# One store of eight output tiles cut into 32 transfers from two queues, with the rows of eight partitions divided differently

## The chip, the core and the metric

The kernel runs on one core of a Trainium2 chip. The core has a matrix engine (TensorE, PE in the profile), two engines for elementwise work (VectorE, DVE, and ScalarE, ACT), a programmable engine (GpSimd, POOL), a queue processor (SyncE, SP), and 16 DMA engines that carry data between the chip's memory (DRAM) and the on-chip memory SBUF, which has 128 partitions. Products are accumulated in a second on-chip memory, PSUM. The metric is the time of one launch in microseconds (us), lower is better; a median of a few runs is given.

## What is computed

`x` has 16 x 1024 rows of 512 floats, `weight` is 512 x 768, `gamma` has 512 entries (all ones here) and `eps` is 1e-5.

```python
rms = np.sqrt(np.mean(x ** 2, axis=-1, keepdims=True) + eps)
x_norm = x / rms * gamma
return np.matmul(x_norm, weight).astype(np.float32)
```

The kernel flattens `x` to 16,384 rows. It reads 16,384 x 512 x 4 B = 33.6 MB, and writes 16,384 x 768 x 4 B = 50.3 MB.

## The kernel before

**Tiles.** The 16,384 rows are 128 tiles of 128 rows; a tile has one row in each partition. For a tile, GpSimd casts the rows to bf16, the tile is turned (by TensorE with an identity, line 230, and copied out of PSUM by VectorE, line 239; for some tiles by VectorE's own 32x32 transposes, line 271), TensorE multiplies it with the bf16 weights (line 300), and ScalarE (even tiles, line 279) or VectorE (odd tiles, line 281) scales the 768 results of each row by the row's 1/rms on their way from PSUM into an output buffer `ot`. The row's sum of squares is formed beside this by ScalarE (line 196).

**Groups and buffers.** Output tiles are gathered in groups of eight. `ot` has three buffers of eight tiles; group g uses buffer g % 3. So the first tile of a group can be written only when the store of the group three before has landed. Groups 1 to 13 (tiles 8 to 111) are each stored by one transfer of eight tiles, 3,072 KB. At the two ends groups are cut smaller: tiles 112 to 127 leave as 4, 4, 4, 2 and 2 tiles.

**How a store lies in memory.** `rows` (line 140) gives partition p a stretch of consecutive rows of the output, so the eight tiles of a group are, in each partition, 8 x 768 floats = 24,576 bytes in one piece in DRAM, and also one piece in `ot`. A store of a group is 128 such pieces.

**Order and queues.** The program is written as a list of operations in one order (class `Order`). `emit` (line 39) walks the list once, works out which earlier operations each one has to wait for, and issues each to its engine's own queue with those waits ahead of it. A transfer gets a semaphore of its own, or takes over that of an earlier transfer that its queue is known to have seen finished (lines 64 to 70). All stores and the first loads are issued by SyncE, later loads by ScalarE; GpSimd issues no transfer. `store` (line 288) is called after each tile's scaling and issues a transfer when the last tile of its group has been written. A queue is in order: SyncE, while it waits for the tiles of one store, issues nothing else.

**The end of the program.** The transfers that nobody in the program waits for (the last stores) are collected; ScalarE waits for all of them but the last one (lines 438 to 440), and the last store, of tiles 126 and 127, is issued by SyncE behind everything else (lines 441 to 446). The program ends when all have landed.

```python
def store(i):
    first, n = o_first[i], o_size[i]
    s = first // OG % 3
    if i == first + n - 1:
        src = ot[s][:, first % OG:first % OG + n, :]
        order.transfer(SP, lambda: SP.dma_start(out=rows(out, first, n), in_=src), reads=cells("ot", s, first % OG, n))
```

Of the kernel before, what the change touches and what calls it, by code (L numbers as in the profile page):

```python
# [20 lines left out]
class Order:  # L21
# [17 lines left out]
    def emit(self):  # L39
        nc = self.tc.nc  # L40
        streams = {id(e): n for n, e in enumerate((nc.tensor, nc.vector, nc.scalar, nc.gpsimd, nc.sync))}
        writer, readers = {}, {}
        known = [dict() for _ in streams]
        clocks, needs, place, slot_of, slots = [], [], [], {}, []
        count = [0] * len(streams)
        for n, (proc, engine, _, reads, writes) in enumerate(self.ops):
            at = streams[id(engine)]
            if proc is None:
                me, turn = ("transfer", n), 1
            else:  # L50
                count[at] += 1
                me, turn = at, count[at]
            written = {writer[cell] for cell in reads + writes if cell in writer}
            read = {d for cell in writes for d in readers.get(cell, ())}
            need = []
            for d in sorted(written | read, reverse=True):
                who, when = place[d]
                if who == me and (engine is nc.tensor or d not in written):
                    continue
                if known[at].get(who, 0) < when:  # L60
                    need.append(d)
                    for k, v in clocks[d].items():
                        known[at][k] = max(known[at].get(k, 0), v)
            if proc is None:
                free = [k for k, d in enumerate(slots) if known[at].get(("transfer", d), 0)]
                if free:
                    slots[free[0]] = n
                else:
                    slots.append(n)
                slot_of[n] = ("slot", slots.index(n))  # L70
            clock = dict(known[at])
            clock[me] = turn
            place.append((me, turn))
            clocks.append(clock)
            needs.append(need)
            for cell in reads:
                readers.setdefault(cell, []).append(n)
            for cell in writes:
                writer[cell], readers[cell] = n, []
        awaited = {d for need in needs for d in need}  # L80
        seen = {who for clock in known for who in clock}
        last = [n for n, (me, _) in enumerate(place) if me not in seen and not isinstance(me, int)]
        sems, marks, done = {}, {}, {}
        for n in range(len(self.ops)):
            me = slot_of.get(n, place[n][0])
            if n in slot_of or n in awaited:
                if me not in sems:
                    sems[me] = self.tc.alloc_semaphore(f"done{len(sems)}")
                done[me] = done.get(me, 0) + (16 if n in slot_of else 1)
                marks[n] = (sems[me], done[me])  # L90
        for n, (proc, engine, issue, _, _) in enumerate(self.ops[:-1]):
            for d in needs[n]:
                engine.wait_ge(*marks[d])  # L93
            ins = issue()
            if n in marks:
                ins.then_inc(marks[n][0], 16 if n in slot_of else 1)
        return [marks[n] for n in last if n < len(self.ops) - 1], self.ops[-1][2]
# [3 lines left out]
def kernel(  # L101
# [8 lines left out]
    nc = tc.nc  # L110
    PE, DVE, ACT, POOL, SP = nc.tensor, nc.vector, nc.scalar, nc.gpsimd, nc.sync
    order = Order(tc)
# [5 lines left out]
    out = out.flatten_outer_dims()  # L118
    N, D = x.shape
    _, O = out.shape  # L120
    K = D // P
    NT = N // P
    NP = NT // 2
    XG, OG = 16, 8
# [15 lines left out]
    def rows(ap, i, n):  # L140
        base, t = (i - i % OG, OG) if OG <= i < XG else (x_first[i], x_size[i]) if i < OG else (i - i % XG, XG) if i < 2 * XG else (i - i % (2 * XG), 2 * XG)
        return ap[base * P:(base + t) * P, :].rearrange("(p t) d -> p t d", t=t)[:, i - base:i - base + n, :]

    def sb(name, shape, dtype):
        return nc.alloc_sbuf_tensor(name, shape, dtype).ap()
# [14 lines left out]
    ot = [sb(f"ot{n}", [P, OG, O], F32) for n in range(3)]  # L160
# [7 lines left out]
    def cells(name, slot, i, n=1):  # L168
        return [(name, slot, t) for t in range(i, i + n)]
# [115 lines left out]
    def accumulator():  # L285
        return next(turns) % 3

    def store(i):
        first, n = o_first[i], o_size[i]
        s = first // OG % 3  # L290
        if i == first + n - 1:
            src = ot[s][:, first % OG:first % OG + n, :]
            order.transfer(SP, lambda: SP.dma_start(out=rows(out, first, n), in_=src), reads=cells("ot", s, first % OG, n))

    def hold(lhsT, cell):
# [21 lines left out]
    def finish_tile(i, a, engine):  # L317
        s = i // OG % 3

        before = [("ot", s, i % OG - 1)] if i == o_first[i] + o_size[i] - 1 else []  # L320
        scale(engine, ot[s][:, i % OG, :], ops[a][:, :O], rstd[:, i:i + 1],
              [("ops", a, 0), ("ops", a, 1), ("rstd", i)] + before, [("ot", s, i % OG)])
        store(i)
# [158 lines left out]
```

## Time and profile before

| What | Value |
|---|---|
| Median of 3 runs | 208.95 us (208.85 to 216.69) |
| The profiled execution's own time | 209.07 us |
| Span from its first to its last instruction | 207.1 us |
| PE, DVE, ACT, POOL busy, share of the span | 94%, 72%, 70%, 29% |
| Granted PE clock, mean | 0.993 |
| Moved by DMA | 85.62 MB, 413 GB/s over the span |
| Packets on SyncE's queue, on ScalarE's queue | 4,320 and 1,732 |
| Last GpSimd instruction begins | 171.44 us |
| Store of tiles 104 to 111 is issued | 177.86 us |
| Last store is issued, lands | 200.40 us, 206.16 us |

The profile is one execution. Times within it count from its first instruction. "Issued" is the time at which the queue's processor handed the transfer over; "landed" is when the transfer's semaphore reached its full count. That semaphore is raised in 16 steps, and the trace has the time of each. The trace also has each DMA packet with its start, length and size, but not which of the 16 DMA engines carried it. The DMA share in a table of windows is the time of all packets that began in the window, divided by the window and by 16, so 1.00 means that all 16 engines are at work and 0.06 that one is. An engine that is busy in the page need not be the one that others wait for; the chain of waits and the windows show that.

### The profile page before, as it was taken

To read this page: it belongs to the slowest core of one execution; us is meant where nothing else is said; L and a number is where in the kernel's file an instruction comes from. 1 tells how busy PE (TensorE), PEld (TensorE's weight loads), DVE (VectorE), ACT (ScalarE), POOL (GpSimd) and SP (SyncE) were. 2 spreads that over 40 slices of the span, in tenths; PEclk is the share of its full clock that TensorE was granted. 3 is DMA by queue.
4 is the path that set the end of the run, shared out by engine and by line. 5 is a ranking of instruction groups with operands and counts; after the bars stand their busy time and mean duration, and the time that the engine had idled before them with its cause. 6 is when DMAs were issued, how large, how long until landed. Compare 5 with 4: busy or idle time off the path is not lost.

```text
span 207.1 us, 2794 instructions
## 1 busy us (share of the span) xinstructions
PE 194.7 (94%) x1236; PEld 72.7 (35%) x717; DVE 149.5 (72%) x255; ACT 144.3 (70%) x343; POOL 60.0 (29%) x34
## 2 busy tenths in 40 slices
PE   7789999999999999999999999999999989999940
PEld 1233434343334334433344333443343324333310
DVE  0446556999579975999579975999569964999530
ACT  4598898777777687777777687676949758683310
POOL 2156752157006340065105170060604224000000
PEclk9999999999999999999999999999999999999997
DMA  6999999999999999999999999999999999999992
GB/s 222 402 434 453 370 419 420 426 461 407 437 429 423 449 419 440 419 434 429 432 449 411 430 434 423 445 423 437 413 424 445 427 440 435 423 437 394 394 412 120
DMA packets 6064, 85.62 MB, mean 413 GB/s; under 512 B 674, under 2 KB 676, under 8 KB 1828
## 3 DMA queue, kind: packets, MB, share of 16 engines
q1 hardware_dynamic: 4320, 60.30, 68.9%
q10 hardware_dynamic: 1732, 25.17, 28.5%
q8 instruction: 7, 0.11, 0.2%
q14 instruction: 5, 0.04, 0.0%
HBM read 35.13 MB, written 50.33 MB: 413 GB/s over the span
## 4 chain that ended last, share of the span: by engine, by line
PE 71%; DMA 17%; DVE 5%; SPq 1%; issue 1%; POOL 1%; ACT 0%; ACTq 0%
PE ps L300 63%; DMA out_dram<-ot 12%; PE ps L230 8%; DMA xt<-in_x_dram 5%; DVE ot L281 2%; DVE xTq L271 2%; DVE xT L239 1%; POOL xb L188 1%; SPq L345 0%; ACT ot L279 0%; SPq L177 0%; DVE rstd L203 0%; SPq L477 0%; ACTq L93 0%; SPq L436 0%
## 5 line engine op out<-in xcount | busy, mean ns | idle before, releaser
L300 PE MATMUL ps<-w_bf,xT 128*128 128x512 bf16 (+1 forms) x800 | 147.9, 326 | 2.1 <-DVE w_bf L281 1.1
L279 ACT ACTIVATE ot<-ps,rstd 128x768 f32<-128x768 f32 x64 | 57.6, 899 | 48.5 <-PE ps L300 37.3
L196 ACT ACTIVATE jk<-xt 128x512 bf16<-128x512 f32 x128 | 78.7, 619 | 1.9 <-DMA xt<-in_x_dram 1.9
L188 POOL CAST xb<-xt 128x2048 bf16<-128x2048 f32 (+3 forms) x21 | 46.4, 2218 | 112.4 <-PE ps L230 69.0
L281 DVE TENSOR_SCALAR ot<-ps,rstd 128x768 f32<-128x768 f32 x64 | 64.8, 1013 | 9.5 <-PE ps L300 8.1
L296 PEld LDWEIGHTS <-xT 128*128 128x128 bf16 x400 | 39.3, 98 | 60.7 <-issue 52.8
L230 PE MATMUL ps<-ident_f,xb 128*128 128x128 f32 x200 | 54.4, 276 | 0.9 <-POOL xb L188 0.9
L239 DVE COPY xT<-ps 128x1024 bf16<-128x1024 bf16 (+1 forms) x53 | 34.5, 654 | 24.2 <-PE ps L230 22.5
L271 DVE STREAM_TRANSPOSE xTq<-xq 32x256 f32<-32x256 f32 x112 | 48.8, 435 | 3.4
L230 PEld LDWEIGHTS ps<-ident_f,xb 128*128 128x128 f32 x200 | 28.3, 143 | 46.6 <-issue 43.3
L300 PE MATMUL ps<-w_bf,xTq 128*128 128x512 bf16 x224 | 42.8, 326 | 0.0
L196 ACT ACTIVATION_READ_ACCUMULATOR jk<-xt 128x1 f32 x128 | 24.4, 190 | 0.0
L296 PEld LDWEIGHTS <-xTq 128*128 128x128 bf16 x112 | 11.0, 98 | 14.5 <-issue 14.5
L260 POOL CAST xq<-xt 128x2048 bf16<-128x2048 f32 x7 | 13.3, 1893 | 0.0
L203 DVE RECIPROCAL rstd<-rms 128x8 f32<-128x8 f32 (+3 forms) x20 | 3.9, 193 | 8.1 <-ACT rms L201 7.9
L201 ACT ACTIVATE rms<-ssq,eps_sb 128x8 f32<-128x8 f32 (+3 forms) x20 | 6.0, 300 | 0.6
L300 PE MATMUL ps<-warm 128*128 128x512 bf16 x10 | 4.5, 588 | 1.4 <-DVE eps_sb L354 1.4
L279 ACT ACTIVATE w_bf<-w_f,g_sb 128x768 bf16<-128x768 f32 x2 | 1.9, 935 | 1.8 <-DMA w_f<-in_weight_dram 1.8
L377 DVE COPY g_sb<-ps 128x4 f32<-128x4 f32 x1 | 0.2, 163 | 3.2 <-PE ps L371 3.2
L341 ACT ACT_TABLE_LOAD x1 | 1.3, 1283 | 1.5 <-SPq L436 1.5
L281 DVE TENSOR_SCALAR w_bf<-w_f,g_sb 128x512 bf16<-128x512 f32 (+2 forms) x3 | 1.4, 482 | 1.2 <-DMA w_f<-in_weight_dram 1.2
L371 PEld LDWEIGHTS ps<-ident_f,g_row 2*128 2x128 f32 x2 | 0.3, 200 | 2.6 <-issue 2.6
(10 smaller groups left out, 2.0 us busy)
## 6 DMA issues: line engine op xcount, KB each, us to landing
out_dram<-ot SPq DMA_DIRECT2D x13, 3072.0 KB, 22.7
xt<-in_x_dram ACTq DMA_DIRECT2D x12, 2048.0 KB, 18.8
xt<-in_x_dram SPq DMA_DIRECT2D x3, 2048.0 KB, 18.2
out_dram<-ot SPq DMA_DIRECT2D x4, 1536.0 KB, 10.9
out_dram<-ot SPq DMA_DIRECT2D x3, 768.0 KB, 6.8
w_f<-in_weight_dram SPq DMA_DIRECT2D x2, 768.0 KB, 5.9
xt<-in_x_dram SPq DMA_DIRECT2D x2, 512.0 KB, 5.4
xt<-in_x_dram SPq DMA_DIRECT2D x1, 1024.0 KB, 9.5
```

The lines of the kernel that those rows point to most:

```text
L188: run(POOL, lambda: POOL.tensor_copy(out=xb[s][:, i % 8:i % 8 + n, :], in_=src), of, cells("xb", s, i % 8, n))
L196: run(ACT, lambda: ACT.activation(out=jk[j], in_=src[:, 0, :], func=AF.Square, accum_out=ssq[:, i:i + 1]), of, [("jk", j), ("ssq", i)])
L201: run(ACT, lambda: ACT.activation(out=rms[:, s], in_=ssq[:, s], func=AF.Sqrt, scale=1.0 / D, bias=eps_sb), [("ssq", t) for t in range(i, i ...
L203: run(DVE, lambda: DVE.reciprocal(out=rstd[:, s], in_=rms[:, s]), [("rms", i)], [("rstd", t) for t in range(i, i + n)])
L230: run(PE, lambda: PE.transpose(out=tp[b][:, t, h, :], in_=words[:, lo:lo + P], identity=ident_f), cells("xb", s, j % 4 * 2 + t) + ["ident" ...
L239: run(DVE, lambda: DVE.tensor_copy(out=dst[:, t:t + n, :], in_=src[:, t:t + n, :]), [("tp", b)], cells("xT", j % 4, t, n))
L260: run(POOL, lambda: POOL.tensor_copy(out=xq[s], in_=src), of, [("xq", s)])
L271: run(DVE, lambda: DVE.transpose(out=dst, in_=src), [("xq", s)], [("xTq", s)])
L279: run(ACT, lambda: ACT.mul(out=dst, in_=src, mul=r), reads, writes)
L281: run(DVE, lambda: DVE.tensor_single_scalar(out=dst, in_=src, scalar=r, op=mybir.AluOpType.mult), reads, writes)
L296: run(PE, lambda: PE.ldweights(lhsT), [cell])
L300: run(PE, lambda: PE.add_instruction(mybir.InstMatmult(name=nc.get_next_instruction_name(), engine=mybir.EngineType.PE, ins=[PE.lower_ap(r ...
```

## The change

The store of one group, tiles 104 to 111 (`first == NT - 24`, group 13), is no longer one transfer of SyncE. A new function `spread` issues 32 transfers, 16 on SyncE and 16 on GpSimd, in eight rounds. A round p takes:

- on SyncE, the seven partitions p, p+4, ..., p+24, whole rows (7 x 24,576 B);
- on GpSimd, the partition p+28, the first 384 of the 768 columns of each of its eight rows (8 pieces of 1,536 B);
- on GpSimd, the eight partitions p+64, p+68, ..., p+92, whole rows (8 x 24,576 B);
- on SyncE, the partition p+28, the other 384 columns (8 pieces of 1,536 B).

Over the rounds p = 0 to 3 and 32 to 35 this covers all 128 partitions once. The partitions that are taken apart are 28 to 31 and 60 to 63. In `emit`, a transfer that GpSimd issues always gets a semaphore of its own. All other stores, the loads and the computation are as before, and so is the number of bytes.

```diff
             if proc is None:
                 free = [k for k, d in enumerate(slots) if known[at].get(("transfer", d), 0)]
-                if free:
+                if free and engine is not nc.gpsimd:
                     slots[free[0]] = n
                 else:
                     slots.append(n)
...
+    def spread(dst, src, held):
+
+        def part(engine, p, n, cols=slice(0, O)):
+            at = slice(p, p + 4 * n - 3, 4)
+            order.transfer(engine, lambda: engine.dma_start(out=dst[at, :, cols], in_=src[at, :, cols]), reads=held)
+
+        for p in (0, 1, 2, 3, 32, 33, 34, 35):
+            part(SP, p, 7)
+            part(POOL, p + 28, 1, slice(0, O // 2))
+            part(POOL, p + 64, 8)
+            part(SP, p + 28, 1, slice(O // 2, O))
+
     def store(i):
         first, n = o_first[i], o_size[i]
         s = first // OG % 3
         if i == first + n - 1:
             src = ot[s][:, first % OG:first % OG + n, :]
+            if first == NT - 24:
+                spread(rows(out, first, n), src, cells("ot", s, first % OG, n))
+                return
             order.transfer(SP, lambda: SP.dma_start(out=rows(out, first, n), in_=src), reads=cells("ot", s, first % OG, n))
```

## The prediction, made before the changed kernel was run

> **What bounds the kernel now.** I read the page's busy shares and slices first, then the end of the chain of waits, then windows of the last microseconds.
>
> ```profile
> PE 194.7 (94%) x1236; PEld 72.7 (35%) x717; DVE 149.5 (72%) x255; ACT 144.3 (70%) x343; POOL 60.0 (29%) x34
> ...
> PE   7789999999999999999999999999999989999940
> ...
> POOL 2156752157006340065105170060604224000000
> PEclk9999999999999999999999999999999999999997
> DMA  6999999999999999999999999999999999999992
> ```
>
> TensorE and the DMA engines are both full almost throughout, the clock is granted, and GpSimd (POOL) is empty in the last six slices. With two candidates the end has to be looked at by itself. The chain ends with matmuls of line 300 to 199.06 and this:
>
> ```profile
> 199.09 1.02 DVE ot L281
> ```
>
> The last tile is scaled at 200.11, its store is issued at 200.40 and lands 5.8 us later, at 206.16. What are these 5.8 us? Windows after the issue (stretch, length, busy time of PE, PEld, DVE, ACT, POOL, PE clock, DMA share, GB/s):
>
> ```profile
> 200.00:203.20 3.20, 0.00 (x0) 0.00 (x0) 0.10 (x1) 0.00 (x0) 0.00 (x0) 1.00 1.02 419
> 203.60:204.60 1.00, 0.00 (x0) 0.00 (x0) 0.00 (x0) 0.00 (x0) 0.00 (x0) 0.83 0.06 25
> 204.60:205.60 1.00, 0.00 (x0) 0.00 (x0) 0.00 (x0) 0.00 (x0) 0.00 (x0) 0.50 0.06 25
> ```
>
> Until 203.2 all sixteen DMA engines work; from 203.6 to 205.6 the share is 0.06, one sixteenth: **one DMA engine alone holds up the end**. The semaphore steps agree: fifteen of the last store's land at 203.60 to 203.79, the sixteenth at 206.16, 2.37 us later. The lag is old: behind the fifteenth it was 1.31 us in the store issued at 142.43, 1.94 at 166.14, 2.23 at 177.86. From one landing to the next (176.08, 183.65, 191.19) this engine needed 7.57 us for its share of 3,072 KB, the fifteenth (174.46, 181.71, 188.96) 7.25. What a lighter load on it can give is these **2.37 us, 1.1%**, and no more; a measurement of this kernel tells about 2% from no change.
>
> **The change, part by part.** The store as it was, issue and landing:
>
> ```profile
> 177.86 0.33 SPq L293 DMA_DIRECT2D out_dram<-ot  x1
> ...
> out_dram<-ot SPq DMA_DIRECT2D x1, 3072.0 KB, 13.3
> ```
>
> Its buffer (group 13, buffer 1) is not used again, so no compute instruction waits for it, before or after; if it lands late, only the end is late. I follow the DMA engines in three classes, and take for this that partitions 28 to 31 and 60 to 63 are the late engine's share.
>
> (1) That engine gives up 7.57 us and gets an eighth of eight rows: 16 pieces of 1,536 B. The packet records show 121 ns for 3,072 B, so 0.061 us each, 0.98 us in all. It is 6.6 us less loaded, far over its lag, and falls in with the others.
>
> (2) Seven engines keep their 24,576 B a round on SyncE and get the same 0.98 us on top. Idle time hides it: in every store seven engines are early (store of 142.43: seven steps to 165.49, eight from 166.34 to 166.62, one at 167.93), and near 191 and again before 196 they run dry:
>
> ```profile
> 195.00:195.90 0.90, 0.90 (x8) 0.24 (x3) 0.00 (x0) 0.72 (x1) 0.00 (x0) 1.00 0.75 314
> ```
>
> With 16 engines at 0.75 over 0.9 us, some 3.6 engine-us are idle; the count of packets under way falls to 8. If that cover were gone, this class would end 0.98 us later and cap the gain at 1.4 us. Their feed keeps pace if two SyncE issues take under the 1.03 us of work that a round brings. SyncE's nearest row:
>
> ```profile
> 2.47 2.49 SPq L177 DMA_DIRECT2D xt<-in_x_dram  x5
> ```
>
> Five issues back to back, 0.50 us each, of which 0.33 is the instruction in later rows. The new ones have 7 or 8 pieces where those have 128. I take 0.42 us, between 0.33 and 0.50: 16 of them last until 177.86 + 6.7 = 184.6. Behind them in SyncE's queue stands the store of tiles 112 to 115, issued at 184.07 before: 0.5 us late (none at 0.33; 1.8 us at 0.50).
>
> (3) Eight engines carry partitions 64 to 127 and get this store from GpSimd alone. GpSimd is free: its last cast begins at 171.44 and ends at 173.33. But a round takes it two transfers, of c us each, and brings each engine 0.91 us of work (24,576 B; 912 ns in 1,540 of 1,664 packets). These engines have earlier work until about 181.15 (their landings of 181.36 to 181.71, less the 0.48 us by which the late engine's last landing, 206.16, follows its last packet, 205.68). After that they starve in part, until the next full-width store arrives. **c is the unknown of this change**: no GpSimd transfer is in the trace. From below, SyncE's issue of the same operation, 0.33 us. From above, GpSimd's usual instruction:
>
> ```profile
> L260 POOL CAST xq<-xt x7: 1893/1893/1894, 30.3 to 171.4; 128x2048 bf16<-128x2048 f32 x7
> ...
> 10.04 1.04 POOL L188 CAST xb<-xt 128x1024 bf16<-128x1024 f32 x1 [4.51 <-DMA xt<-in_x_dram]
> ```
>
> Those work through 1,024 to 2,048 elements a partition, and the shortest casts (512 elements) take 0.61. A transfer has 8 pieces to describe, so I take the middle of the two short casts, **c = 0.8**. From issue to first packet I use 1.0 us (first load: issued 0.94, first packet 1.98; the store of 194.93: engines back at work at 195.9). The eight engines' 24,576 B arrive at 177.9 + 1.6 k + 1.0 = 180.5, 182.1, 183.7, 185.3 and so on, the next store at 184.6 + 1.0 = 185.6. They work 181.15 to 182.06, 182.1 to 183.0, 183.7 to 184.6, and from 185.3: 1.44 us idle. About 0.2 of it would have been idle before 195.9 anyway. So this class ends 1.24 us later than the fifteen did.
>
> ScalarE's 32 further waits at the end cost nothing: a passed wait is 0.02 us (a chain row of line 93), 0.6 us in all, and ScalarE has nothing else to do from 198.68 to the landing at 206.16.
>
> The sum, on the profiled execution's own time (209.07; 1.97 of it outside the span): 209.07 - 2.37 + 1.24 = 207.94. That execution is 0.12 above the median of the runs, 208.95; I say **207.9 us**, a gain of 0.5%.
>
> [...]
>
> **Rivals.** (A) The sum above, with c from 0.33 to 1.2: at 0.4 there is no idle time and all of 2.37 goes, 206.6; at 1.2 the arrivals are 2.4 us apart and the eight engines are idle for 2.4 us, which gives it all back. Own range 206.5 to 208.9.
>
> (B) Slower: GpSimd feeds too slowly. Place: the eight engines after 181. It decides from c = 1.2, where idle time passes 2.37 + 0.2. Up to c = 1.6 the loss stays under 1.2 us, since the later stores fill the gaps; beyond, the last of the 16 transfers itself arrives after the rest. At c = 1.9 that is 177.9 + 30.4 + 1.0 = 209.3, with 0.91 of work 210.2 against 205.68: +4.5, so 213.5. For it: the median cast is 1.89. Against: the pieces are few.
>
> (C) The pieces land elsewhere. If GpSimd's 8-row transfers fell on the same eight engines that SyncE uses, those would get 7.27 us more, of which idle time hides some 2: 203.4 + 0.98 + 7.27 - 1.8 = 209.9 against 205.68, +4.2, or 213.1. No row tells which engine takes which row of a short transfer.
>
> (D) It doesn't do what it says: the late engine is another one. No packet record names its engine. Then the late one keeps its 7.57 us and adds 0.98, since it has no idle time: 209.9; if it is one of the eight of (3), its backlog to 183.2 covers most of the starving and it loses 0.5: 209.5.
>
> **Chances.** A 0.60, B 0.20, C 0.08, D 0.12. Faster by over 2% (under 204.8) asks for more than the lag there is: 0.01. Slower by over 2% (over 213.1): B from c = 1.87, 0.05, and half of C, 0.04, with 0.01 for hidden costs of the new queue: 0.10. Within 2%: 0.89. The range goes from all of the lag gone, 206.5, to GpSimd at its usual cast, 213.5.
>
> **What would show it.** In the changed profile: the lone 0.06 after 203.6 is gone; the last store's sixteen steps land within some 0.5 us, or a group of eight is last, which is B's sign. GpSimd's sixteen transfers would be a row between 178 and 191 with c as their spacing, the DMA share from 181 to 186 near 0.85, and SyncE's store of tiles 112 to 115 at 184.6. A last store with one step 2 us behind would show D; seven or eight engines some 6 us behind, C. I would be wrong above all through c, and if the short transfers cost the DMA engines more than their bytes.

## The result: slower by 4%

The changed kernel took 218.05 us (median of 4 runs, 217.82 to 218.17), the kernel before, on the same chip, 209.28 us (median of 4, 208.85 to 216.69). The ratio is **1.0425, 95% interval 1.0397 to 1.0453**. Forecast were 207.9 us and a range from 206.5 to 213.5. The 216.69 is an execution in the chip's slower state and is not in the ratio.

The profiled execution took 218.09 us, its span is 216.3 us. From its page, the lines that answer to those shown of before:

```profile
PE 194.3 (90%) x1212; PEld 72.8 (34%) x717; DVE 149.6 (69%) x255; ACT 143.7 (66%) x343; POOL 68.3 (32%) x50
...
PE   7899999999999999999999899998999999999000
...
POOL 3236660552023600633032600624033607700000
PEclk9999999999999999999999999999999999999955
DMA  6999999999999999999999999999999996546994
...
q0 software_dynamic: 512, 1.67, 2.1%
...
L292 POOL DMA_DIRECT2D out_dram<-ot x16 | 8.3, 527 | 6.2 <-DVE ot L281 6.2
```

TensorE's busy time is that of before (194.3 against 194.7). New are a dip of the DMA row, "6546", over some 20 us, and three slices at the end without TensorE where before there was one. GpSimd's sixteen transfers took 8.3 us together to issue, 527 ns each. The chain of waits still ends with the last tile, but what follows it is now much longer:

```profile
200.57 0.02 issue
200.60 1.02 DVE ot L281
```

The tile is scaled at 201.62 (before 200.11), its store lands at 215.20 (before 206.16). Why so late is told by SyncE's own timeline (start, length, queue, line, operation, count; a merged row covers the time from the first to the last of its issues):

```profile
168.57 0.33 SPq L308 DMA_DIRECT2D out_dram<-ot  x1
179.37 17.81 SPq L292 DMA_DIRECT2D out_dram<-ot  x16
197.23 5.07 SPq L308 DMA_DIRECT2D out_dram<-ot  x5
```

Sixteen short issues keep SyncE from 179.37 to 197.18, 1.11 us each. The store of tiles 112 to 115, ready long before, goes out at 197.23; in the kernel before it went at 184.07:

```profile
184.07 0.33 SPq L293 DMA_DIRECT2D out_dram<-ot  x1
```

GpSimd's timeline of the changed kernel ends sooner:

```profile
179.65 8.29 POOL L292 DMA_DIRECT2D out_dram<-ot  x16 [6.22 <-DVE ot L281]
```

What the DMA engines do meanwhile is in windows of the changed kernel (stretch, length, busy PE, PEld, DVE, ACT, POOL, then PE clock, DMA share, GB/s):

```profile
180.00:184.00 4.00, 3.95 (x27) 1.62 (x16) 3.69 (x8) 3.08 (x8) 4.00 (x9) 1.00 0.54 199
184.00:188.00 4.00, 4.00 (x28) 1.59 (x16) 3.84 (x8) 3.04 (x10) 3.94 (x8) 1.00 0.55 213
188.00:192.00 4.00, 3.95 (x27) 1.44 (x15) 3.80 (x7) 1.40 (x2) 0.00 (x0) 1.00 0.50 199
192.00:196.00 4.00, 4.00 (x26) 1.17 (x12) 3.27 (x6) 1.30 (x2) 0.00 (x0) 1.00 0.46 190
196.00:200.00 4.00, 3.95 (x26) 1.21 (x13) 1.43 (x2) 1.60 (x2) 0.00 (x0) 1.00 0.63 256
200.00:204.00 4.00, 0.56 (x4) 0.06 (x1) 1.02 (x1) 0.20 (x1) 0.00 (x0) 1.00 1.05 439
```

and of the kernel before, for the second and fourth of these:

```profile
184.00:188.00 4.00, 4.00 (x28) 1.58 (x16) 3.80 (x9) 2.36 (x5) 0.00 (x0) 1.00 0.95 409
...
192.00:196.00 4.00, 4.00 (x27) 1.22 (x13) 2.27 (x3) 1.72 (x2) 0.00 (x0) 1.00 0.94 396
```

**Half of the DMA engines stand idle from about 182 to 198.** The share is a half, and the rate is a half too (199 GB/s at 0.54, against 409 at 0.95). In the packet records at most eight packets of data are under way at a time from 183.2 to 198, mostly eight or seven (a ninth for 0.13 us in all; from 182 to 183.2 it is mostly nine). The engines at work carry SyncE's short transfers, and GpSimd's as well: had the 8-row transfers of GpSimd gone to the other eight, these would have shown. Then the wide store comes, all sixteen work at 1.05, and the end is one lone engine again:

```profile
213.80:214.80 1.00, 0.00 (x0) 0.00 (x0) 0.00 (x0) 0.00 (x0) 0.00 (x0) 0.50 0.05 18
```

Fifteen of the last store's steps land at 213.44 to 213.62, the sixteenth at 215.20. The lag that the change was about is still there: 1.58 us, where it was 2.37.

**Where the 9 us are.** The last landing moved by 215.20 - 206.16 = 9.04 us, in four parts along the path:

| Part | before | after | difference |
|---|---|---|---|
| store of tiles 104 to 111 issued | 177.86 | 179.37 | +1.51 |
| from there to the store of tiles 112 to 115 | 6.21 | 17.86 | +11.65 |
| from there to the fifteenth step of the last store | 19.72 | 16.39 | -3.33 |
| from the fifteenth step to the sixteenth | 2.37 | 1.58 | -0.79 |

The first part lies ahead of the change: in this execution the tiles had already fallen behind before the split; why, and whether the other three did, is open. The second is the loss. The third says how much of a late issue is hidden: before, the engines had 3.3 us of earlier work in front of these stores; now they have none.

### The profile page after: what moved, and what is told of

It is laid out like the page before. It is cut to its first block, busy times and chain, and to the rows that moved or that the text cites. A ratio compares the mean times of both kernels' runs of the same rounds, so it can differ in the third digit from the quotient of the medians.

```text
span 216.3 us, 2817 instructions
## 1 busy us (share of the span) xinstructions
PE 194.3 (90%) x1212; PEld 72.8 (34%) x717; DVE 149.6 (69%) x255; ACT 143.7 (66%) x343; POOL 68.3 (32%) x50
## 4 chain that ended last, share of the span: by engine, by line
PE 59%; DMA 29%; DVE 2%; issue 1%; ACT 1%; SPq 1%; POOL 0%; ACTq 0%
PE ps L315 52%; DMA out_dram<-ot 24%; PE ps L230 7%; DMA xt<-in_x_dram 4%; DVE ot L281 1%; ACT ot L279 1%; POOL xb L188 0%; SPq L360 0%; SPq L177 0%; DVE xT L239 0%; ACT jk L196 0%; SPq L492 0%; ACTq L93 0%; DVE xTq L271 0%; SPq L451 0%
## 5 line engine op out<-in xcount | busy, mean ns | idle before, releaser
L315 PE MATMUL ps<-w_bf,xT 128*128 128x256 bf16 (+1 forms) x783 | 145.7, 325 | 3.5 <-ACT ot L279 2.3
L315 PE MATMUL ps<-w_bf,xTq 128*128 128x256 bf16 (+1 forms) x217 | 41.8, 324 | 0.4
L292 POOL DMA_DIRECT2D out_dram<-ot x16 | 8.3, 527 | 6.2 <-DVE ot L281 6.2
```

The costliest lines, as they stand in the source:

```text
L292: order.transfer(engine, lambda: engine.dma_start(out=dst[at, :, cols], in_=src[at, :, cols]), reads=held)
L315: run(PE, lambda: PE.add_instruction(mybir.InstMatmult(name=nc.get_next_instruction_name(), engine=mybir.EngineType.PE, ins=[PE.lower_ap(r ...
```

## Experiments

Four questions: what do SyncE's short issues cost by themselves, what do GpSimd's transfers add, what slows an issue or an engine, and which engine is late. All kernels are made from the changed one or from the one before; the kernel before took 208.79 us beside the first four, 208.98 beside the next four, 209.53 and 209.25 (medians of 7) beside the later ones. A time given without an interval is one execution. "The next store" is that of tiles 112 to 115, "the fifteenth" and "the sixteenth" are steps of the last store.

### SyncE's short transfers alone

The changed kernel without GpSimd's 8-row transfers; GpSimd's eight half rows stay. Partitions 64 to 127 of tiles 104 to 111 are not written.

```diff
-            part(POOL, p + 64, 8)
```

> The changed kernel without GpSimd's eight 8-row transfers (partitions 64 to 127 of tiles 104 to 111 are not written); SyncE's 16 and GpSimd's 8 half-row transfers stay. Theory 1 (GpSimd's 8-row transfers fall on the same eight DMA engines as SyncE's, these have to carry the whole group alone, and their backlog holds up SyncE's issues): SyncE's 16 issues take 0.75 us or less each, the store of tiles 112 to 115 is issued at 186 to 191.5 instead of 197.2, the time is 205 to 210. Theory 2 (a short transfer is slow to issue on SyncE by itself, 1.1 us each): the 16 issues still take about 17.8 us, that store is issued at 197 and the time stays at 215 to 218.

Measured: 210.78 us. Timeline of SyncE and two windows of this run:

```profile
177.72 12.14 SPq L292 DMA_DIRECT2D out_dram<-ot  x16
189.90 10.68 SPq L307 DMA_DIRECT2D out_dram<-ot  x5
```

```profile
184.00:188.00 4.00, 3.95 (x27) 1.73 (x17) 3.80 (x9) 2.29 (x5) 0.00 (x0) 1.00 0.38 150
188.00:192.00 4.00, 4.00 (x27) 1.18 (x13) 3.81 (x7) 0.90 (x1) 0.00 (x0) 1.00 0.59 239
```

The sixteen issues are steady, 0.68 us for a half row and 0.70 to 0.77 for seven rows (the first 0.91), also where the DMA share is down to 0.38. That is not a wait for the engines; it is their own price, 12.2 us together. The next store goes out at 189.90, and the fifteenth lands at 206.29.

Timed again against the kernel before:

> The run without GpSimd's 8-row transfers again, timed against the kernel before: SyncE's sixteen short transfers alone cost 0.8 to 1.1%, since the store of tiles 112 to 115 is issued 5.8 us late and some 4 us of that are hidden by the engines' earlier work.

Measured: ratio 1.0149, 95% interval 1.0094 to 1.0203. More than expected at its middle (the runs spread from 210.67 to 213.34), the sign is certain: **the SyncE half of the change loses by itself.**

### A hold without any short transfer

Is a late issue really the loss? The kernel before, with nothing split, but with two stores held back until tile 122 has been scaled:

```diff
+            held.append((rows(out, first, n), src, cells("ot", s, first % OG, n)))
+        if not NT - 16 <= i < NT - 6:
+            while held:
+                dst, src, read = held.pop(0)
+                late = cells("ot", s, i % OG) if i == NT - 6 else []
+                order.transfer(SP, lambda dst=dst, src=src: SP.dma_start(out=dst, in_=src), reads=read + late)
```

> The kernel before, but the stores of tiles 112 to 115 and of 116 to 119 are held until tile 122 has been scaled (about 196.1 us); no short transfers, no GpSimd transfer, nothing left out. Hold theory: the DMA engines run dry from about 189 to 197, the work that then remains (14.6 us) starts 1 us after the issue; the last store lands at 212 to 213.5 and the time is 214.5 to 216, with little of the late engine's lag left. Rival: a late issue is absorbed by the engines' backlog and the changed kernel's idle engines come from what the short transfers cost the engines themselves: 208.5 to 210.

Measured: 221.34 us, but this execution had fallen behind long before: in the store issued at 162.17 fifteen steps land by 175.74 and the sixteenth at 183.67, so tile 122 was scaled only at 202.1. Its last store landed 16.29 us after the release at 202.15. So it was run again, with repetitions:

> The stores of tiles 112 to 119 held until tile 122 is scaled, without any short transfer, again: in the first run of it the loads had fallen behind from 84 us on, and the release came at 202.15 instead of about 196. Hold theory: release at 196 to 196.5, DMA engines idle from about 191 to 197, last store landed 16 to 16.4 us after the release (212 to 213), time 214 to 215.5, lag of the late engine gone. Rival (a late issue is absorbed): 208.5 to 210.

Measured: 212.61 us, ratio 1.0142, interval 1.0099 to 1.0186. The timeline of SyncE from 177 and three windows:

```profile
178.40 0.33 SPq L300 DMA_DIRECT2D out_dram<-ot  x1
...
194.05 7.22 SPq L300 DMA_DIRECT2D out_dram<-ot  x5
```

```profile
184.00:188.00 4.00, 4.00 (x29) 1.66 (x17) 3.84 (x8) 2.37 (x7) 0.00 (x0) 1.00 0.90 387
188.00:192.00 4.00, 4.00 (x27) 1.28 (x13) 3.77 (x8) 1.51 (x2) 0.00 (x0) 1.00 0.06 25
192.00:196.00 4.00, 4.00 (x27) 1.18 (x12) 2.78 (x4) 1.18 (x2) 0.00 (x0) 1.00 0.35 147
```

Tile 122 was ready at 194.05, not at 196, so my time was too high by that much; the engines ran dry (0.06), and the last store landed at 210.33, 16.28 us after the release. All its steps are within 0.18 us: after a pause in which the late engine caught up, the lag is gone. A hold alone makes idle DMA engines and a late end; the rival, that a late issue is absorbed, falls.

The same distance shows in every run in which a hold had let the engines run dry:

| Run | next store issued | fifteenth (without a lag: last) step | distance |
|---|---|---|---|
| SyncE's short transfers alone | 189.90 | 206.29 | 16.39 |
| hold alone | 194.05 | 210.33 | 16.28 |
| the changed kernel | 197.23 | 213.62 | 16.39 |
| ScalarE's one transfer (below) | 197.99 | 214.36 | 16.37 |
| GpSimd's one transfer (below) | 199.74 | 216.12 | 16.38 |

**The end is the issue of that one store plus 16.3 to 16.4 us**, whatever had held it.

### What makes the hold longer: the other half, issued in another way

With GpSimd's 8-row transfers the hold was 17.86 us instead of 12.18. In the next two the rows of partitions 64 to 127 leave as one transfer of 64 rows, issued ahead of the short ones; first by GpSimd.

```diff
+        order.transfer(POOL, lambda: POOL.dma_start(out=dst[64:, :, :], in_=src[64:, :, :]), reads=held)
...
-            part(POOL, p + 64, 8)
```

> The changed kernel with partitions 64 to 127 as one GpSimd transfer of 64 rows, issued first; SyncE's 16 and GpSimd's 8 half-row transfers as in the changed kernel. Theory 1: 64 rows spread over all sixteen engines, 4 each (3.6 us), so the eight carry 3.6 + 8.3 = 11.9 us and not 15.5, are done by about 193, and the store of tiles 112 to 115 is issued at 188 to 193: time 208 to 212. Theory 2: it is issued at 197, time 215 to 218. Theory 3 (the number of GpSimd transfers slows SyncE's issuing, whichever engines carry them): with 9 in place of 16, SyncE's issues get faster only in part, that store is issued at about 194, time 213 to 215.

Measured: 219.41 us, next store at 199.74. Windows:

```profile
180.00:184.00 4.00, 3.95 (x27) 1.60 (x16) 3.69 (x8) 2.97 (x7) 3.81 (x8) 1.00 0.99 252
184.00:188.00 4.00, 4.00 (x29) 1.65 (x17) 3.80 (x8) 3.58 (x11) 0.85 (x2) 1.00 0.96 235
188.00:192.00 4.00, 3.95 (x26) 1.40 (x14) 3.83 (x7) 0.90 (x1) 0.00 (x0) 1.00 0.39 84
```

SyncE's issues took 2.98, 2.31, 2.44, 2.23 and 1.27 us up to 193, then 0.68 and 0.73 as without GpSimd. So the hold does not need GpSimd's 8-row transfers, and a single transfer over all engines doesn't set SyncE free either. (GpSimd's eight half rows are still there, but they were also there in the run without the 8-row transfers, where no issue waited.) The windows say something else too: all engines are busy (0.99), but at 252 GB/s instead of 400 and more. I come back to that.

Then the same transfer issued by ScalarE, whose queue the page lists as `hardware_dynamic` like SyncE's, where GpSimd's is `software_dynamic` (`POOL` becomes `ACT` in the line above):

> As the run with partitions 64 to 127 in one GpSimd transfer, but that transfer is issued by ScalarE, so its packets come by a hardware queue. Theory A (SyncE's short transfers are slow to issue while packets of GpSimd's software queue are on the engines): the 16 issues take 0.68 to 0.77 us each, the store of tiles 112 to 115 is issued at 189 to 192, time 210 to 213. Theory B (any other queue's packets do it): issues of 2 to 3 us as before, that store at 196 to 200, time 215 to 219.

Measured: 217.73 us, next store at 197.99; issues of 1.61, 3.63, 2.58 and 2.53 us, then 0.68 to 0.86. **It isn't GpSimd's queue that holds SyncE.** While other transfers are under way on the engines that the short ones go to, a short issue takes up to 3.6 us. They need not be another queue's: in the run with several forms, below, SyncE's own transfers are the only ones and an issue takes up to 3.49. What it waits for there no record shows.

### The next stores taken off SyncE

The changed kernel, with the stores of tiles 112 to 125 issued by ScalarE, so that SyncE's hold can't reach them.

```diff
+            queue = ACT if NT - 16 <= first < NT - 2 else SP
+            order.transfer(queue, lambda: queue.dma_start(out=rows(out, first, n), in_=src), reads=cells("ot", s, first % OG, n))
```

> The changed kernel with the four stores between the split one and the last (tiles 112 to 125) issued by ScalarE, so that none of them stands behind SyncE's 16 short transfers. Theory 1: the eight engines still have 15.5 us for the split store and 14.6 us for the rest from 181.2 on, 211.3; the last store lands at 211.8 to 213.8, time 213.5 to 216. Theory 2 (all of the loss is the wait in SyncE's queue): the stores are issued at 184 to 198 as in the kernel before, time 207 to 210.

Measured: 218.00 us, as the changed kernel. The timeline of ScalarE's issues and of SyncE's last two rows:

```profile
184.02 0.35 ACTq L309 DMA_DIRECT2D out_dram<-ot  x1
192.25 0.35 ACTq L309 DMA_DIRECT2D out_dram<-ot  x1
196.21 0.34 ACTq L309 DMA_DIRECT2D out_dram<-ot  x1
199.05 0.34 ACTq L309 DMA_DIRECT2D out_dram<-ot  x1
```

```profile
177.80 20.99 SPq L292 DMA_DIRECT2D out_dram<-ot  x16
209.65 0.34 SPq L309 DMA_DIRECT2D out_dram<-ot  x1
```

The stores are issued early, at 0.35 us each, while SyncE's short ones take up to 1.86. But the one of 199.05 lands at 213.09: nine of its sixteen steps come at 204.09 to 207.40 and seven at 209.88 to 213.09, and seven is the number of engines that each transfer of seven rows goes to (the changed kernel's trace has seven later steps for each). (In the kernel before the same store's steps came at 201.73 to 201.94, and one at 204.30.) So without any hold **the placement puts seven engines 2.5 to 6 us behind the others**, in part by slower engines: the windows of this run from 184 to 204 have 338 to 400 GB/s for a full share, the kernel before some 430. The last store then went out at 209.65, though its tile was scaled at 201.62. By the times, SyncE stood at the end of the block until GpSimd's last transfer had landed, at 208.85; the run with GpSimd's 8-row transfers beside one of SyncE's, below, agrees (landed 202.17, last store issued 202.65, tile scaled 200.02). The total of 218.00 contains this wait. In the changed kernel GpSimd's last transfer landed at 198.32, ahead of the last tile, so there it cost nothing. To free the stores from SyncE therefore brought nothing in this form.

### Full and half widths

GpSimd's eight 8-row transfers as they are, the other half as one transfer of SyncE:

```diff
+        order.transfer(SP, lambda: SP.dma_start(out=dst[:64, :, :], in_=src[:64, :, :]), reads=held)
+        for p in (0, 1, 2, 3, 32, 33, 34, 35):
+            part(POOL, p + 64, 8)
```

> Partitions 0 to 63 as one SyncE transfer, partitions 64 to 127 as GpSimd's eight 8-row transfers; no short transfer on SyncE. If eight engines carry all of GpSimd's rows: they have 181.2 + 3.6 + 7.3 + 14.6 = 206.7 where the kernel before has 203.4, the other eight are done at least 5 us earlier but for the waiting at the last stores, and the time is 210.5 to 213. The store of tiles 112 to 115 is issued at 184. If the placing costs nothing and only SyncE's issuing does: 208 to 209.5.

Measured: 214.79 us. The next store is on time (183.99), the last store's steps spread from 206.04 to 211.53. But from 180 to 196 the share is 0.96 to 1.01 at only 261 to 320 GB/s, and the last store went out 2.6 us after its tile was scaled, so the run shows the placement mixed with slower engines and with the wait at the end of the block. Next, each half as one transfer, so that no placement is left:

```diff
+        order.transfer(SP, lambda: SP.dma_start(out=dst[:64, :, :], in_=src[:64, :, :]), reads=held)
+        order.transfer(POOL, lambda: POOL.dma_start(out=dst[64:, :, :], in_=src[64:, :, :]), reads=held)
```

> Tiles 104 to 111 as two transfers, partitions 0 to 63 from SyncE and 64 to 127 from GpSimd; each spreads 4 rows to all sixteen engines. Neither cause is there: the store of tiles 112 to 115 is issued at 184 in 0.33 us, and the time is 208 to 209.7, as before the change. If the software queue's packets slow every issue on SyncE, that store takes 2 us or more to issue and the time is over 210.

Measured: 217.11 us, 8 us lost, though the packet records show sixteen engines at work where the changed kernel had eight. Two further runs tell the half width from the software queue. First both halves on queues of the hardware kind (`POOL` becomes `ACT`):

> The store of tiles 104 to 111 as two transfers of 64 rows, partitions 0 to 63 on SyncE and 64 to 127 on ScalarE; nothing from GpSimd. If two half-width transfers side by side slow the DMA engines whatever the queue: busy share near 1.0 at 230 to 300 GB/s between 180 and 196, time 215 to 218, as with GpSimd. If GpSimd's software queue slows them: over 390 GB/s throughout and 208.5 to 210.

Measured: 217.23 us.

```profile
184.00:188.00 4.00, 4.00 (x28) 1.62 (x16) 3.84 (x8) 3.84 (x11) 0.00 (x0) 1.00 0.99 270
188.00:192.00 4.00, 4.00 (x27) 1.40 (x14) 3.83 (x6) 1.23 (x2) 0.00 (x0) 1.00 1.15 249
```

Then the whole store by GpSimd, one transfer of 128 rows:

```diff
+        order.transfer(POOL, lambda: POOL.dma_start(out=dst[:, :, :], in_=src[:, :, :]), reads=held)
```

> The store of tiles 104 to 111 as one transfer of 128 rows issued by GpSimd; all else as in the kernel before. If the half width is what slows the engines: over 390 GB/s, 208.5 to 210. If the software queue does: under 330 GB/s at a share near 1.0 until about 195, and 213 to 218.

Measured: 209.07 us.

```profile
184.00:188.00 4.00, 4.00 (x29) 1.63 (x17) 3.81 (x8) 2.36 (x5) 0.00 (x0) 1.00 0.97 415
188.00:192.00 4.00, 4.00 (x27) 1.27 (x14) 3.77 (x8) 0.92 (x2) 0.00 (x0) 1.00 0.99 421
```

The software queue costs nothing (209.07 us against 209.25), the half width costs 8 us: at a share of 0.97 the one moves 415 GB/s, the other 270 at 0.99 and 249 at 1.15. In the packet records the 24,576-byte packets of partitions 64 to 127 take 1.82 us in the median on ScalarE's queue and 1.47 on GpSimd's, where those of a full-width store take 0.912. Why the packets of a half take longer, no run here shows.

### What a short issue costs

First several forms in place of the split, on SyncE alone (and small loads, which belong to the last question):

```diff
+        step(0, 16, 1)
+        step(16, 8, 1)
+        step(24, 7, 1)
+        step(31, 1, 1, slice(0, O // 2))
+        step(31, 1, 1, slice(O // 2, O))
+        for p in range(32, 36):
+            step(p, 8, 4)
+        for p in range(64, 68):
+            step(p, 16, 4)
```

> No GpSimd transfer. SyncE stores tiles 104 to 111 by 13 transfers of different forms: 16, 8 and 7 adjacent partitions, two half rows of one partition, 4 x 8 partitions and 4 x 16 partitions in steps of four. And the eight small loads of 8 to 1 rows again behind the store of tiles 96 to 103. If the step of four is what makes an issue 0.72 us: 8 and 7 adjacent rows take 0.33, both forms with steps 0.7. If it is the use of fewer than 16 engines: 16 rows take 0.33 with and without steps, 7 and 8 rows 0.7 with and without. If neither, all take about 0.7. The late engine: again the fifth, so a late step in the loads of 5 to 8 rows and in none of fewer. Time 208.5 to 211.5.

Measured: 217.09 us, well over what was expected. 16 and 8 adjacent rows took 0.33 and 0.31 us, the next three issues 2.26, 3.49 and 1.70 while the engines worked off the first ones. After them 8 rows four partitions apart took 0.63 to 0.65, 16 rows so 0.59 to 0.85 and the last of these 2.25. So the two causes were mixed; the next run separates them, at the start of the program, where no engine has a backlog: twelve loads, then twelve stores, three of each form.

> The kernel before with 24 small SyncE transfers at its very start, twelve loads and then twelve stores to an unused array, three each of: 8 adjacent rows of 1 KB; 8 rows four partitions apart, 1 KB each; 8 rows four partitions apart, 7 KB each; one row as seven pieces of 1 KB. If the step between the rows is what makes a short issue of the changed kernel cost 0.7 us, the second and third form take 0.6 to 0.75 us each and the first 0.25 to 0.35; if the bytes, only the third is long; if stores are dear and loads not, all of the later twelve. If all stay under 0.35, the 0.7 us came from the engines' load at that place. The time itself only grows by the delayed start, 8 to 14 us.

The loads, form by form, in SyncE's timeline (three of 8 adjacent rows; the last two of three with 8 rows of 1 KB four apart; three with 7 KB; three of one row, which the compiler made one piece of 7 KB and not seven):

```profile
0.97 1.09 SPq L370 DMA_DIRECT2D pr<-in_x_dram  x3
...
2.90 1.30 SPq L370 DMA_DIRECT2D pr<-in_x_dram  x2
...
4.24 1.95 SPq L370 DMA_DIRECT2D pr<-in_x_dram  x3
...
6.24 1.00 SPq L370 DMA_DIRECT2D pr<-in_x_dram  x3
```

Each issue, without the gaps: adjacent 0.29, four apart 0.62 with 1 KB and 0.62 with 7 KB, one piece 0.25 (the first of some forms is longer: 0.40, 0.75, 0.41). The stores gave the same (0.29, 0.60 to 0.62, 0.25). **For eight rows the step of four partitions doubles the price of an issue; 1 or 7 KB a row and the direction make no difference.** Why a half row, eight pieces of one partition, cost 0.68 in the run with SyncE's short transfers alone, was not taken apart. The total of 221.15 us holds the delayed start (the first own load at 13.27 instead of 0.94) and nothing else of interest.

If the step is dear, are adjacent rows better? The changed kernel with neighbouring partitions in each transfer:

```diff
-            at = slice(p, p + 4 * n - 3, 4)
+            at = slice(p, p + n)
...
-        for p in (0, 1, 2, 3, 32, 33, 34, 35):
+        for p in range(0, 64, 8):
```

> The changed kernel with neighbouring partitions in each short transfer (7 adjacent rows on SyncE, the eighth in two halves, 8 adjacent rows on GpSimd). If the step of four partitions is what holds SyncE: sixteen issues of 0.3 us, the store of tiles 112 to 115 issued at 184 to 186, and the time is set by the eight loaded engines alone, 211 to 213. If the other queue's backlog on those engines holds it: first issues 0.3 us, later ones over 1 us, the store of tiles 112 to 115 not before 190, time 214 to 218.

Measured: 229.61 us, worse than either theory. SyncE's timeline and two windows:

```profile
180.48 27.31 SPq L292 DMA_DIRECT2D out_dram<-ot  x16
207.84 7.41 SPq L308 DMA_DIRECT2D out_dram<-ot  x5
```

```profile
180.00:184.00 4.00, 4.00 (x29) 1.67 (x17) 3.72 (x8) 2.41 (x6) 3.24 (x7) 1.00 0.58 137
184.00:188.00 4.00, 4.00 (x28) 1.56 (x16) 3.80 (x7) 3.97 (x11) 4.00 (x8) 1.00 0.47 113
```

The first issue is short (0.35), the third already 2.64. Eight engines are busy as in the changed kernel, but move 113 GB/s where those moved 213: SyncE's packets of 24,576 B take 1.93 us in the median and up to 3.69, where those of the changed kernel take 0.912. So with the step of four the engines stayed near their full rate (213 GB/s at a share of 0.55, the kernel before 409 at 0.95), at twice the price of an issue. In this run most of the hold of 27.4 us is waiting: sixteen issues at the 0.35 us of the first would take 5.6 (an estimate from that issue). In the changed kernel waiting is the smaller part: of 17.9 us the issues' own price, as the run with SyncE's transfers alone has it, is 12.2.

### Which engine is late

The kernel before, with eight small loads of one to eight adjacent rows (256 B each) behind the store of tiles 96 to 103. The semaphore of each has as many steps of its own as the load has rows, so I take each row to go to another engine.

```diff
+            if first == NT - 32:
+                for m in (1, 2, 3, 4, 5, 6, 7, 8):
+                    probe(m)
```

> The kernel before with eight small extra loads into unused memory (1 to 8 rows of 256 B), issued by SyncE directly behind the store of tiles 96 to 103. Their steps land as each DMA engine gets through its share of that store, so they tell which engines a short transfer uses. If the late engine is the eighth, as the change has it: in the loads of 2 to 7 rows no step is 1.3 us or more behind the others, in that of 8 rows one is. If it is one of the first seven: a late step from some smaller number of rows on. If it is among the other eight: none in any. Issue on SyncE: Theory 1, with no GpSimd transfers about, 0.35 to 0.75 us each; Theory 2, about 1.1 us each. Time 208.5 to 210.

Measured: 209.3 us. A step 1.5 us and more behind the others (183.97) appears first in the load of **five** rows. In the run with the several forms above, which asked in the reverse order, it is again there with 8, 7, 6 and 5 rows (183.79, 183.99, 184.19, 184.38) and missing with four and fewer. So the late engine is the fifth in the order in which short transfers fill them. The eighth, which the change took for the late one, lands with the early ones (180.24). The changed kernel's own trace agrees that the late engine is one of the first seven: in the first transfer of seven rows six steps land by 182.83 and the seventh at 184.88. Which partitions an engine serves in a full store no run shows.

## Why the prediction was wrong, point by point

- **What bounds the end**: right. One DMA engine lags, and 2.37 us of the end were its alone; the probes show it again. That a lighter load on it gives them back was not tried.
- **Step (1), the relieved engine is the late one**: wrong. It is the fifth, not the eighth, which is rival D. The lag of 1.58 us in the changed kernel is that of one of the seven engines which still have all their rows. So none of the 2.37 us could come from a lighter load, even had all else gone as I put it. The prediction gave this 0.12 and stated that no record names an engine. Its three classes, and which partitions belong to each, were its assumption; no run shows which partitions an engine serves.
- **Step (2), SyncE's issue at 0.42 us, next store at 184.6**: the largest error. The term was taken from loads of 128 adjacent rows. Its parts: 0.76 us with the gaps for the new forms by themselves (12.2 us for sixteen, not 6.7), and 1.11 in the changed kernel, 17.9 us. The prediction saw the queue behind it and what a late store would do, but ended its bounds at 0.50, from one row of another form; no rival priced a longer hold, and the largest price of any, 213.5, was for GpSimd. With 0.76 its own sum gives the next store at 177.86 + 12.2 = 190.1, and the run with SyncE's transfers alone has 189.90.
- **Step (3), the eight engines fed by GpSimd**: the class doesn't exist; the 8-row transfers went to the engines that the short ones of SyncE use. That is rival C, at 0.08. Its price of +4.2 counted only the load. With these transfers on the same engines SyncE's hold also grew, from 12.18 us to 17.86, and both end at about the same time: the eight engines are through at about 198, the next store is issued at 197.2.
- **c, said to be the unknown of this change**: 0.53 us and not 0.8, inside the bounds, and of no weight. GpSimd's first packet started 1.22 us after its issue began (179.65 to 180.87; 1.26 to 1.53 in three other runs), where the prediction used 1.0 from SyncE's transfers; the next transfer was issued 0.51 to 0.64 us after the one before. The care went into the wrong term: both ends of c were priced, the issue of SyncE got one row.
- **ScalarE's extra waits cost nothing**: right. From the last landing to the end of the execution's time it was 2.89 us in the changed kernel, 2.91 before.
- **The signs named beforehand**: those of the rivals came, of the sum's only GpSimd's row (179.65 to 187.94). "A last store with one step 2 us behind would show D": 1.58. "Seven or eight engines some 6 us behind, C": seven, 2.5 to 6 us, in the run with ScalarE's stores. A DMA share near 0.85 from 181 to 186: 0.54. The store of tiles 112 to 115 at 184.6: 197.23.

What makes an issue wait while other transfers are under way is open; so is how much the changed kernel would lose by placement alone, without SyncE's wait at the end of the block.

## What to carry to other kernels

Splitting a transfer changed three things here that the byte count doesn't show: the price of each issue on its in-order queue (0.62 us for 8 rows four partitions apart, 0.29 for 8 adjacent ones; ask for the row of that very form), which DMA engines get the pieces (eight of sixteen in the changed kernel, at a share of 0.46 to 0.55 from 180 to 196), and how many partitions one transfer spans (415 GB/s with 128, 249 to 270 with two transfers of 64 side by side). Before relieving a slow engine, find it: eight small loads of one to eight rows showed its place in the order, in a run of 209.3 us beside 208.79 without them. And a wide store that stands behind short ones is the price to work out first: in five runs the end was its issue plus 16.3 to 16.4 us.

## What the runs showed of the hardware that I had not expected

- An issue of 8 rows four partitions apart costs SyncE 0.62 us, of 8 adjacent rows 0.29, of 128 adjacent rows 0.33; with other transfers under way on the same engines up to 3.6 us. Wide stores can wait too: 2.07 and 2.37 us in the run with a half each from SyncE and GpSimd. In the kernel before, stores issued while earlier ones were under way took 0.33.
- GpSimd issues a transfer of 8 rows four apart in 0.52 us, less than SyncE, and one of 128 rows in 0.67; and a full-width store from it ran at 415 GB/s, as SyncE's (409 in the same window).
- Two half-width stores side by side moved 218 to 301 GB/s between 180 and 196 at a DMA share of 0.88 to 1.15, where one full-width store moved 393 to 436; adjacent rows on eight engines moved 73 to 157. In these runs a busy share near 1.0 therefore didn't say how much the engines moved (249 or 415 GB/s): the GB/s beside it did.
- In five runs the last five stores ended 16.3 to 16.4 us after the first of them was issued, where most of the engines had run dry before; and the lag of the late engine is gone after a pause: 0.16 us from first to last step in the run with GpSimd's one transfer, 0.18 in the hold alone.
- The late engine's lag is not a constant of the kernel: 2.37 us in the execution profiled before, 1.15 in that of SyncE's transfers alone, and over 7 us (183.67 behind 175.74) in the first of the two holds, where the whole program had fallen behind with it.
